# Softmax weights times values as one plain float32 product in both attentions of a two-layer hybrid step, with even and odd key tiles in the two column halves of TensorE

## The chip, the cores and the metric

The kernel runs on one core of a Trainium2 chip. The metric is the device time of one execution, in microseconds (us). The engines are called by their names in the profile: PE is TensorE's matrix multiply and PEld its weight load, DVE is VectorE, ACT is ScalarE, POOL is GpSimd, SP issues the transfers.

## What is computed

The program is one step of a two-layer backbone on 1024 latent tokens and 128 context tokens (1152 rows of width 1024). In every layer one input projection feeds three head groups, whose outputs go through an output projection, a LayerNorm, a SwiGLU feed-forward block (FFN) and another LayerNorm. The two attentions are what the change touches:

```python
# differential attention: 4 heads, queries and keys of 2 x 32, values of 64
s = jnp.einsum('bqhcd,bkhcd->bhcqk', qb, k).astype(F32) * scale
p = jax.nn.softmax(s, axis=-1)
a = p[:, :, 0] - lam * p[:, :, 1]
return jnp.einsum('bhqk,bkhd->bqhd', a.astype(v.dtype), v)
...
# latent attention (MLA): 8 heads, values of 64 made from a latent of 128
s = (jnp.einsum('bqhd,bkhd->bhqk', qn, k_nope)
     + jnp.einsum('bqhd,bkd->bhqk', qr, k_rope)).astype(F32) * scale
p = jax.nn.softmax(s, axis=-1)
return jnp.einsum('bhqk,bkhd->bqhd', p.astype(v.dtype), v)
```

The latent tokens see 1152 keys (9 tiles of 128), the context tokens only their own 128 (1 tile). All is float32.

## The kernel before

Most products are made in a split form: each float32 operand is written as a high and a low part in the type `fp32r` (helper `split`, lines 121 to 125: one engine copies the high part, another subtracts it from the source), and `mm3` (lines 127 to 130) adds three products: high times high, low times high, high times low. A product in `fp32r` is one matmul record on PE; a product in plain float32 is two records, one behind the other (the program has 296 matmuls on line 801, the trace 592 records).

A layer runs through these stages, each with its own tile pools: the input projection and the state-space part; the differential attention; the latent attention; output projection, norms and FFN. In a stage the work is written as a list of steps with due times (`weave`, which sorts them), and the tile framework's scheduler then sets the final order on each engine. The constants `LAG_D`, `AV_LAG_D`, `LAG_M`, `GSTEP`, `AV_LAG` are such due times, and the names ending in `BUFS` are buffer counts.

Differential attention, `diff_unit`: a unit is a head and two query tiles (256 queries; a unit of one tile for the context). `front` makes the scores of one tile and one of the two components (line 702, three matmuls of 384 keys into PSUM tile `s`, of which there are two), their maximum on DVE (line 714), the exponential on ACT (line 717, tile `e`), and after the second component the combination of both on POOL or DVE (lines 781 to 784). `tr` transposes `e` on PE (line 791, PSUM tile `t`, two buffers) and ACT copies the result to `aT` (line 794). `av` (line 801) multiplies the nine key tiles, one after the other, all into the same 64 rows of `o`, in plain float32: the values `vd` are the stationary operand (64 columns), `aT` streams 256 columns. `back_tokens` (line 809) transposes the 64-row result back with the identity.

Latent attention, `mla_unit`: a unit is again a head and two query tiles, 32 of them in a layer and 8 single context tiles. The scores are three-fold split products (line 702, tile `s`, 96 rows), with maxima on DVE (line 739), exponentials on ACT (line 748), and the division by the sum on POOL (line 959). `tr` transposes (line 967) and then splits the weights into `eh` and `el`: for three of five groups of two key tiles, ACT casts `eh` and DVE subtracts `el`, both from PSUM; for the groups 2 and 6, ACT copies to `ef`, DVE casts `eh`, POOL subtracts `el`. `av` (lines 986 and 987) uses stationary tiles `vv` of 128 columns, 64 for the high and 64 for the low part of the values, and streams first `eh` and then `el`, so each key tile takes two matmuls of 256 columns. At the end ACT copies the lower half of the result and DVE adds the upper (lines 990 and 991). `values` (line 899) makes `vv` and splits it on ACT and DVE.

Of the kernel before, what the change touches and what calls it, by code (L numbers as in the profile page):

```python
# [78 lines left out]
EL_BUFS = 4  # L79
EF_BUFS = 2  # L80
# [17 lines left out]
def dit_step(ctx, tc, ins, outs):  # L98
# [15 lines left out]
    def dma(out, in_):  # L114
        return sp.dma_start(out, in_)  # L115
# [31 lines left out]
    dma(ident, ins["ident"])  # L147
    mhalf = T(con, [128, 1], F32, "mhalf")
# [234 lines left out]
    for l in range(L):  # L383
# [375 lines left out]
        def diff_unit(h, t0, n, st):  # L759
# [46 lines left out]
            def back_tokens():  # L806
                o = v["o"][:, 256:256 + n * 64].rearrange("p (i d) -> p i d", d=64)
                for i in range(n):
                    pe.transpose(o[:, i], v["ob"][:, i * 128:(i + 1) * 128], ident[:64, :64])
# [89 lines left out]
        def values(half, kts, big):  # L899

            if half not in vv:
                vv[half] = T(mw["p"] if half else Vp, [128, 10, 4, 2, 64], F32R, f"vv{half}")
# [5 lines left out]
            p3 = ps.rearrange("p k (h d) -> p k h d", d=64)  # L908
            v = vv[half][:, kts[0]:kts[0] + n]
            split(v[:, :, :, 0, :], v[:, :, :, 1, :], p3, vec)  # L910
# [33 lines left out]
        def mla_unit(bi):  # L944
# [17 lines left out]
            def tr(g0):  # L962
# [6 lines left out]
                eh = T(mw["p"], [128, 512], F32R, "eh", EL_BUFS)  # L969
                el = T(mw["p"], [128, 512], F32R, "el", EL_BUFS)  # L970
                if g0 in (2, 6):
                    ef = T(mw["p"], [128, 512], F32, "ef", EF_BUFS)
                    act.copy(ef[:, :gn * w], pt[:, :gn * w])
                    split(eh[:, :gn * w], el[:, :gn * w], ef[:, :gn * w], pool, vec)
                else:
                    split(eh[:, :gn * w], el[:, :gn * w], pt[:, :gn * w], vec)
                v[g0] = (eh, el)

            def av(g0):
                if g0 == 0:  # L980
                    v["o"] = T(ps_pool[0], [128, 512], F32, "x", 1)[:, :w]
                eh, el = v[g0]
# [780 lines left out]
```

## Time and profile before

| | us |
|---|---|
| median of 3 runs | 3709.5 (3709.39, 3709.50, 4253.26) |
| the profiled execution's own time | 3713.83 |
| its span in the trace | 3711.8 |
| differential attention, layer 0 and layer 1 (first transpose on line 791 to first on line 967) | 263.0 and 228.9 |
| latent attention, layer 0 and layer 1 (first transpose on line 967 to last matmul on line 987) | 310.3 and 309.7 |

The busy shares of the engines are averages over stages with different limits, so the stages are read one by one. A matmul record lasts from when it is issued until its result is written, and records overlap: the cost of a matmul in a stream is the distance from its start to the start of the next, not its duration. An engine counts as busy during the whole record, so a busy PE can still be waiting for part of the time.

### The profile page before, as it was taken

The numbers are of one execution on the slowest core, as the hardware profiler recorded it, in microseconds if no ns is written. First come the engines' busy times: TensorE is split into PE (matmuls) and PEld (weight loads), VectorE is DVE, ScalarE is ACT, GpSimd is POOL, SyncE is SP. The second block draws the span as 40 slices with busy tenths as digits, with TensorE's granted clock in tenths as the row PEclk, the third lists the DMA queues.
The fourth block names the chain that finished last, engine by engine and source line by source line (L and its number), as shares of the span: only waits on it lengthen the run. The fifth ranks groups of instructions, "written<-read, shape, count | busy, mean of one in ns | idle before, by whom it ended". The sixth has DMA issues, their size and how long they took to land.

```text
span 3711.8 us, 54836 instructions
## 1 busy us (share of the span) xinstructions
PE 3432.9 (92%) x19856; PEld 3153.0 (85%) x19856; DVE 2124.9 (57%) x4285; ACT 1596.7 (43%) x3261; POOL 1540.0 (41%) x1583
## 2 busy tenths in 40 slices
PE   5898888999999999999998987899999999999997
PEld 2786447888988999999998965588889999999996
DVE  7865557888578465334465667688865321222336
ACT  2315556677563444444143265567755211111122
POOL 4561336677566555555034424467732101010013
PEclk8998999999999999999999988999999999999998
DMA  8665320011634333222135550001142211111112
GB/s 250 192 186 155 87 75 24 18 33 38 204 98 98 96 115 119 78 79 78 56 124 163 154 129 20 27 23 29 41 157 86 69 41 43 48 33 52 45 52 90
DMA packets 261694, 325.01 MB, mean 88 GB/s; under 512 B 65168, under 2 KB 206896, under 8 KB 261168
## 3 DMA queue, kind: packets, MB, share of 16 engines
q1 hardware_dynamic: 261424, 321.51, 29.6%
q8 instruction: 157, 2.57, 0.3%
q14 instruction: 113, 0.93, 0.1%
HBM read 261.71 MB, written 59.64 MB: 87 GB/s over the span
## 4 chain that ended last, share of the span: by engine, by line
PE 63%; DVE 11%; ACT 7%; DMA 5%; POOL 5%; issue 4%; SPq 1%; DVEq 0%; ACTq 0%; POOLq 0%
PE mm L130 14%; PE mm L129 14%; PE mm L128 13%; PE s L702 6%; PE t L801 3%; PE t L967 2%; POOL aa L255 2%; ACT e L717 1%; PE x L986 1%; PE t L791 1%; PE x L987 1%; DVE dm L714 1%; ACT e L748 1%; DVE mm L739 1%; SPq L115 1%
## 5 line engine op out<-in xcount | busy, mean ns | idle before, releaser
L128 PE MATMUL mm<-hh,wh 128*128 128x384 f32 x2784 | 947.0, 340 | 16.0 <-ACT wh L122 7.6
L130 PE MATMUL mm<-hh,wl 128*128 128x384 f32 x2784 | 945.7, 340 | 12.4 <-DVE wl L125 12.2
L129 PE MATMUL mm<-hl,wh 128*128 128x384 f32 x2784 | 944.8, 339 | 0.1
L128 PEld LDWEIGHTS mm<-hh,wh 128*128 128x128 f32 x2784 | 528.5, 190 | 19.0 <-ACT wh L122 9.5
L130 PEld LDWEIGHTS mm<-hh,wl 128*128 128x128 f32 x2784 | 528.3, 190 | 18.6 <-DVE wl L125 18.4
L129 PEld LDWEIGHTS mm<-hl,wh 128*128 128x128 f32 x2784 | 528.6, 190 | 0.5 <-POOL hl L125 0.4
L125 POOL TENSOR_TENSOR fl<-sg,fh 128x384 fp32r<-128x384 f32 x132 | 153.2, 1160 | 814.3 <-ACT fh L122 814.3
L122 ACT CAST wh<-wr 128x1024 fp32r<-128x1024 f32 (+2 forms) x302 | 239.9, 795 | 544.5 <-PE mm L129 489.7
L255 POOL TENSOR_TENSOR aa<-aa,at 128x256 f32<-128x256 f32 x392 | 328.0, 837 | 289.6 <-ACT at L254 264.1
L702 PE MATMUL s<-ks,qs 96*128 96x384 f32 (+2 forms) x1600 | 383.7, 364 | 56.7 <-ACT e L717 42.2
L125 DVE TENSOR_TENSOR wl<-wr,wh 128x1024 fp32r<-128x1024 f32 (+2 forms) x302 | 297.5, 985 | 231.4 <-ACT wh L122 223.6
L1112 DVE SCALAR_TENSOR_TENSOR acc<-mm,mods,acc 128x384 f32<-128x384 f32 (+2 forms) x640 | 309.4, 511 | 207.1 <-PE mm L130 205.0
L702 PEld LDWEIGHTS s<-ks,qs 96*128 96x128 f32 (+1 forms) x1600 | 276.2, 198 | 103.8 <-ACT e L717 57.7
L1221 DVE TENSOR_TENSOR sg<-mm,sg 128x384 f32<-128x384 f32 x132 | 73.3, 555 | 479.6 <-PE mm L130 453.5
L128 PE MATMUL mm<-fh,wh 128*128 128x384 f32 x960 | 324.3, 339 | 2.5 <-DVE acc L1112 1.9
L130 PE MATMUL mm<-fh,wl 128*128 128x384 f32 x960 | 320.4, 338 | 4.4 <-DVE wl L125 4.4
L129 PE MATMUL mm<-fl,wh 128*128 128x384 f32 x960 | 323.2, 337 | 0.0
L254 ACT ACTIVATE at<-aw,cond 128x256 f32<-128x256 f32 x392 | 199.3, 508 | 258.1 <-POOL aa L255 248.1
L714 DVE TENSOR_REDUCE dm<-s 128x1 f32<-128x1152 f32 (+1 forms) x148 | 181.5, 1237 | 95.5 <-PE s L702 95.2
L739 DVE TENSOR_REDUCE mm<-s 128x1 f32<-128x768 f32 (+2 forms) x264 | 189.4, 719 | 28.7 <-PE s L702 26.0
L959 POOL TENSOR_SCALAR e<-e,mr 128x1152 f32<-128x1152 f32 x144 | 168.8, 1175 | 83.5 <-DVE mr L958 56.6
L125 POOL TENSOR_TENSOR el<-ef,eh 128x512 fp32r<-128x512 f32 x128 | 164.5, 1286 | 80.4 <-DVE eh L124 75.1
(417 smaller groups left out, 6651.7 us busy)
## 6 DMA issues: line engine op xcount, KB each, us to landing
wr<-in_w_gu_dram SPq DMA_DIRECT2D x112, 512.0 KB, 3.6
aw<-in_w_ada_dram SPq DMA_DIRECT2D x224, 128.0 KB, 2.1
wr<-in_w_out_dram SPq DMA_DIRECT2D x48, 512.0 KB, 3.7
wr<-in_w_ada_dram SPq DMA_DIRECT2D x34, 512.0 KB, 5.3
wr<-in_w_dn_dram SPq DMA_DIRECT2D x112, 128.0 KB, 2.1
ks<-kd SPq DMA_DIRECT2D x64, 160.0 KB, 5.1
s_tb<-tbl SPq DMA_DIRECT2D x64, 145.0 KB, 3.4
qs<-qd SPq DMA_DIRECT2D x64, 144.0 KB, 3.9
```

The lines of the kernel that those rows point to most:

```text
L122: act.copy(hi, src)
L125: eng.tensor_tensor(lo, src, raw(hi), op=OP.subtract)
L128: pe.matmul(ps, wh, xh, start=first, stop=False)
L129: pe.matmul(ps, wh, xl, start=False, stop=False)
L130: pe.matmul(ps, wl, xh, start=False, stop=last)
L254: act.activation(t, w, AF.Copy, scale=sc)
L255: pool.tensor_tensor(a, a, t, op=OP.add)
L702: pe.matmul(out, q_ap[a], k_ap[b][:, k0:k0 + out.shape[-1]], start=i == 0, stop=i == len(passes) - 1)
L714: vec.tensor_reduce(m, s, op=OP.max, axis=AX.XY, negate=True)
L739: vec.tensor_reduce(m[:, j:j + 1], s, op=OP.max, axis=AX.XY, negate=True)
L959: pool.tensor_scalar(e[:, :nk], e[:, :nk], r, 1.0, op0=OP.mult, op1=OP.mult)
L1112: vec.scalar_tensor_tensor(acc[ch][m][:, a:b], ps[:, a:b], mods[l][:, gate + m, c:c + 1], acc[ch][m][:, a:b], op0=OP.mult, op1=OP.add)
```

## The change

Both attentions now multiply plain float32 weights with plain float32 values. The two key tiles of a pair go to the two halves of the PE array's columns: the even tile writes rows 0 to 63 of `o`, the odd one rows 64 to 127, each half accumulating for itself. In the latent attention the split of the weights disappears (`eh`, `el` and `ef` become one tile `aT` with one copy from PSUM, on DVE for groups 2 and 8 and else on ACT), and so does the split of the values. In the differential attention the sum of the two halves is made by `back_tokens`: a product with `id2`, two identities on top of each other, takes the place of the transposition. The latent attention still adds the halves on ACT and DVE.

```diff
-EL_BUFS = 4
+EL_BUFS = 6
...
+    id2 = T(con, [128, 64], F32, "id2")
+    vec.tensor_tensor(id2, ident[:, 0:64], ident[:, 64:128], op=OP.add)
...
-                    pe.matmul(o[0:64, 0:w], vd[:, kts[kt], h * 64:(h + 1) * 64], v[kt - j][:, j * w:(j + 1) * w],
-                              start=kt == 0, stop=kt == nkt - 1)
-                ob = v["ob"] = T(X, [64, 256], F32, "ob", 2)
-                act.copy(ob[:, :w], o[0:64, 0:w])
+                    pe.matmul(o[j * 64:(j + 1) * 64, 0:w], vd[:, kts[kt], h * 64:(h + 1) * 64],
+                              v[kt - j][:, j * w:(j + 1) * w], start=kt < 2, stop=kt >= nkt - 2)
+                m = min(nkt, 2) * 64
+                ob = v["ob"] = T(X, [128, 256], F32, "ob", 2)[0:m]
+                act.copy(ob[:, :w], o[0:m, 0:w])
...
-                    pe.transpose(o[:, i], v["ob"][:, i * 128:(i + 1) * 128], ident[:64, :64])
+                    pe.matmul(o[:, i], v["ob"][:, i * 128:(i + 1) * 128], id2[0:m], start=True, stop=True)
...
-                vv[half] = T(mw["p"] if half else Vp, [128, 10, 4, 2, 64], F32R, f"vv{half}")
+                vv[half] = T(mw["p"] if half else Vp, [128, 10, 256], F32, f"vv{half}")
...
-            split(v[:, :, :, 0, :], v[:, :, :, 1, :], p3, vec)
+            act.copy(vv[half][:, kts[0]:kts[0] + n], ps)
...
-                eh = T(mw["p"], [128, 512], F32R, "eh", EL_BUFS)
-                el = T(mw["p"], [128, 512], F32R, "el", EL_BUFS)
-                if g0 in (2, 6):
-                    ef = T(mw["p"], [128, 512], F32, "ef", EF_BUFS)
-                    act.copy(ef[:, :gn * w], pt[:, :gn * w])
-                    split(eh[:, :gn * w], el[:, :gn * w], ef[:, :gn * w], pool, vec)
+                aT = T(mw["p"], [128, 512], F32, "aT", EL_BUFS)
+                if g0 in (2, 8):
+                    vec.tensor_copy(aT[:, :gn * w], pt[:, :gn * w])
                 else:
-                    split(eh[:, :gn * w], el[:, :gn * w], pt[:, :gn * w], vec)
-                v[g0] = (eh, el)
+                    act.copy(aT[:, :gn * w], pt[:, :gn * w])
+                v[g0] = aT
...
-                    st = vv[h // 4][:, kts[g0 + j], h % 4].rearrange("p a d -> p (a d)")
-                    pe.matmul(o, st, eh[:, j * w:(j + 1) * w], start=g0 + j == 0, stop=False)
-                    pe.matmul(o, st, el[:, j * w:(j + 1) * w], start=False, stop=g0 + j == nkt - 1)
+                    kt = g0 + j
+                    pe.matmul(o[j * 64:(j + 1) * 64], vv[h // 4][:, kts[kt], h % 4 * 64:(h % 4 + 1) * 64],
+                              v[g0][:, j * w:(j + 1) * w], start=kt < 2, stop=kt >= nkt - 2)
```

Where the instructions stand. On PE in the latent attention of layer 0, near the end of one unit (`x` is the result of a unit, `s` scores, `vv` the values), the program of before has the two products of each key tile, which the scheduler puts apart as its queue allows:

```order
L986 MATMUL x_5918<-eh_5860,vv_1495_5549 128x256
L987 MATMUL x_5918<-el_5861,vv_1495_5549 128x256
L986 MATMUL x_5918<-eh_5860,vv_1495_5549 128x256
L987 MATMUL x_5918<-el_5861,vv_1495_5549 128x256
L986 MATMUL x_5918<-eh_5873,vv_1495_5549 128x256
L702 MATMUL s_1618_6017<-ks_5374,qs_5343 128x128
L702 MATMUL s_1618_6017<-ks_5375,qs_5343 128x128
L702 MATMUL s_1618_6017<-ks_5374,qs_5344 128x128
L987 MATMUL x_5918<-el_5874,vv_1495_5549 128x256
L986 MATMUL x_5918<-eh_5873,vv_1495_5549 128x256
```

In the changed program, near the end of a unit of the same head, each key tile has one matmul, an even and an odd one together (`x2`), between the projections of the next head (lines 128 to 130), transpositions and scores:

```order
L129 MATMUL t_5895<-qll_2892,wqh_5663 128x384
L130 MATMUL t_5895<-qlh_2891,wql_5664 128x384
L986 MATMUL x_5885<-aT_5883,vv_1496_5551 64x256 x2
L970 MATMUL t_5911<-ident_63,e_1527_5685 128x128
L970 MATMUL t_5911<-ident_63,e_1537_5723 128x128
L986 MATMUL x_5885<-aT_5893,vv_1496_5551 64x256 x2
L704 MATMUL s_1612_5992<-ks_5380,qs_5667 128x384
```

All 1184 matmuls of lines 986 and 987 become 592 on line 986, and these stand in 284 uninterrupted runs: 76 of one key tile, 160 of two, 46 of four, 2 of six. 206 runs come right behind a transposition.

On DVE at the same place, the program of before has subtractions (line 125) and casts (line 124) of the weights among the maxima (line 739):

```order
L125 TENSOR_TENSOR el_5824<-t_5820,eh_5823 128x256
L751 TENSOR_SCALAR ml_1572_5844<-ml_1572_5844 128x1
L958 RECIPROCAL mr_5848<-ml_1572_5844 128x1
L739 TENSOR_REDUCE mm_1584_5896<-s_1583_5892 128x1
L125 TENSOR_TENSOR el_5861<-t_5855,eh_5860 128x512
L742 TENSOR_SCALAR mn_1585_5899<-mm_1584_5896 128x1
L124 CAST eh_5873<-ef_5875 128x512
```

and the changed one has two copies for a unit:

```order
L974 COPY aT_5805<-t_5802 128x256
L753 TENSOR_SCALAR ml_1566_5824<-ml_1566_5824 128x1
L741 TENSOR_REDUCE mm_1575_5865<-s_1574_5861 128x1
L961 RECIPROCAL mr_5828<-ml_1566_5824 128x1
L974 COPY aT_5847<-t_5842 128x512
```

Five instructions of DVE for a unit become two; POOL's two subtractions go without a successor, and ACT has three copies where it had three casts and two copies.

In the differential attention the order on PE hardly moves. The end of the product of one unit before:

```order
L801 MATMUL t_3689<-aT_3646,vd_2888 64x256 x2
L801 MATMUL t_3689<-aT_3666,vd_2888 64x256 x2
L801 MATMUL t_3689<-aT_3671,vd_2888 64x256
L791 MATMUL t_3717<-ident_63,e_839_3557 128x128
L702 MATMUL s_889_3705<-ks_3478,qs_3477 128x384 x3
L702 MATMUL s_895_3724<-ks_3488,qs_3487 128x384 x3
L809 MATMUL t_3689<-ident_63,ob_3699 128x64 x2
```

and in the changed program, with the product that adds the halves in the place of the transposition:

```order
L804 MATMUL t_3691<-aT_3648,vd_2890 64x256 x2
L804 MATMUL t_3691<-aT_3668,vd_2890 64x256 x2
L804 MATMUL t_3691<-aT_3673,vd_2890 64x256
L793 MATMUL t_3719<-ident_63,e_840_3559 128x128
L704 MATMUL s_890_3707<-ks_3480,qs_3479 128x384 x3
L704 MATMUL s_896_3726<-ks_3490,qs_3489 128x384 x3
L814 MATMUL t_3691<-id_2_65,ob_3701 128x64 x2
```

There are 296 such matmuls before and after, in 64 runs before and 65 after; in each of the 32 units of two query tiles eight or nine key tiles stand together.

## Rows read from the trace of the kernel before

**Rows 1.** The page: busy time, share of the span and instructions of each engine.
```profile
PE 3432.9 (92%) x19856; PEld 3153.0 (85%) x19856; DVE 2124.9 (57%) x4285; ACT 1596.7 (43%) x3261; POOL 1540.0 (41%) x1583
```

**Rows 2.** Windows: latent attention (first two), differential attention; busy us, granted clock.
```profile
core 0: us, PE busy (x) PEld busy (x) DVE busy (x) ACT busy (x) POOL busy (x), PEclk, DMA share, GB/s
621.39:931.73 310.34, 289.01 (x1910) 261.64 (x1911) 257.99 (x601) 218.97 (x534) 213.42 (x186) 0.99 0.11 30
2418.83:2728.48 309.65, 286.70 (x1911) 260.24 (x1910) 259.52 (x602) 219.46 (x534) 213.75 (x187) 0.99 0.11 31
358.40:621.39 262.99, 228.06 (x1040) 139.34 (x1039) 157.45 (x263) 141.12 (x269) 105.72 (x69) 0.94 0.22 65
2189.90:2418.80 228.90, 189.99 (x927) 133.85 (x927) 157.31 (x248) 134.99 (x259) 104.64 (x69) 0.92 0.14 36
```

**Rows 3.** Chain that ended last, by line: differential attention layer 0, layer 1, latent attention.
```profile
by line: PE t L801 23.8%; PE s L702 16.7%; PE t L224 11.1%; PE t L791 8.7%; ACT e L717 7.0%; DMA wr<-in_w_ada_dram 6.5%; issue 4.8%; DVE dm L714 4.6%; ACT aT L794 3.5%; SPq L115 1.4%; PE s L128 1.2%; DVE wl L125 1.2%; DVE vv L125 1.1%; PE s
...
by line: PE t L801 18.6%; PE s L702 14.4%; ACT e L717 12.8%; DVE dm L714 10.5%; PE t L791 9.8%; issue 7.3%; DVE e L781 6.2%; ACT aT L794 3.8%; DVE roy L840 3.1%; PE s L128 1.8%; PE s L129 1.4%; PE s L130 1.4%; DVE otok L841 1.3%; DVE wl L77
...
by line: PE s L702 19.4%; PE t L967 12.8%; PE x L986 7.2%; PE x L987 7.1%; issue 6.8%; ACT e L748 5.9%; DVE mm L739 5.7%; DVE eh L124 3.9%; DVE el L125 3.3%; PE t L128 3.1%; ACT eh L122 2.6%; PE t L129 2.4%; PE t L130 2.3%; DVE ks L125 2.2%
```

**Rows 4.** Timeline of PE, float32 product of a differential unit: start, us, instructions.
```profile
484.48 3.67 PE L801 MATMUL t<-aT,vd 128*64 128x256 f32 x16 [0.51 <-ACT aT L794]
488.08 0.79 PE L702 MATMUL s<-ks,qs 128*128 128x384 f32 x3
488.80 0.65 PE L801 MATMUL t<-aT,vd 128*64 128x256 f32 x2
489.38 0.33 PE L791 MATMUL t<-ident,e 128*128 128x128 f32 x1
```

**Rows 5.** Timeline of PE, split product of a latent unit between its scores.
```profile
2599.59 1.21 PE L702 MATMUL s<-ks,qs 96*128 96x384 f32 x6
2600.63 0.28 PE L987 MATMUL x<-el,vv 128*128 128x256 f32 x1
2600.75 0.28 PE L986 MATMUL x<-eh,vv 128*128 128x256 f32 x1
2600.87 0.28 PE L987 MATMUL x<-el,vv 128*128 128x256 f32 x1
2600.99 0.28 PE L986 MATMUL x<-eh,vv 128*128 128x256 f32 x1
2601.11 0.34 PE L702 MATMUL s<-ks,qs 96*128 96x384 f32 x1
```

**Rows 6.** Chain in order of time, latent attention, transpositions: start, us, what.
```profile
2595.08 0.88 PE t L967 x8
...
2601.45 0.44 PE t L967 x4
```

**Rows 7.** Timelines of PE and PEld at line 270: four column groups together, one alone.
```profile
1092.36 0.26 PE L270 MATMUL lnw<-asum,id 128*32 128x16 f32 x8
...
1092.36 0.16 PEld L270 LDWEIGHTS lnw<-asum,id 128*32 128x32 f32 x8 [0.25 <-ACT acc L1159]
...
1241.23 0.23 PE L270 MATMUL lnw<-asum,id 128*32 128x16 f32 x2
...
1241.23 0.14 PEld L270 LDWEIGHTS lnw<-asum,id 128*32 128x32 f32 x2 [0.25 <-issue]
```

**Rows 8.** Groups by shape, latent attention of layer 0, PE: count, busy us, mean ns.
```profile
L702 PE MATMUL s<-ks,qs 96*128 96x384 f32 x534 | 120.5, 352 | 4.7 <-ACT e L748 3.6
L967 PE MATMUL t<-ident,e 128*128 128x128 f32 x584 | 90.0, 277 | 5.6 <-DVE ks L125 1.8 <-DVE el L125 1.6 <-ACT ef L973 0.8
L987 PE MATMUL x<-el,vv 128*128 128x256 f32 x288 | 79.4, 300 | 1.5 <-POOL el L125 1.1 <-DVE el L125 0.2
L986 PE MATMUL x<-eh,vv 128*128 128x256 f32 x288 | 78.7, 296 | 4.7 <-DVE ob L991 3.8 <-DVE eh L124 0.2 <-ACT eh L122 0.2
L128 PE MATMUL t<-qlh,wqh 128*128 128x384 f32 x40 | 14.5, 363 | 1.9 <-ACT ef L973 1.4 <-DVE vv L125 0.4
```

**Rows 9.** Groups by shape of the whole run, DVE, ACT and POOL.
```profile
L124 DVE CAST eh<-ef 128x512 fp32r<-128x512 f32 x128 | 89.3, 697 | 11.1 <-ACT ef L973 10.7
L125 DVE TENSOR_TENSOR el<-t,eh 128x512 fp32r<-128x512 f32 x128 | 87.0, 680 | 10.1 <-ACT eh L122 9.2
L125 DVE TENSOR_TENSOR el<-t,eh 128x256 fp32r<-128x256 f32 x64 | 26.9, 420 | 5.4 <-ACT eh L122 4.0
...
L973 ACT COPY ef<-t 128x512 f32<-128x512 f32 x128 | 75.6, 591 | 40.0 <-PE t L967 37.5 <-PE x L986 1.8
L122 ACT CAST eh<-t 128x512 fp32r<-128x512 f32 x128 | 75.2, 588 | 14.1 <-PE t L967 10.7 <-POOL el L125 1.7 <-PE x L986 0.7
...
L125 POOL TENSOR_TENSOR el<-ef,eh 128x512 fp32r<-128x512 f32 x128 | 164.5, 1286 | 80.4 <-DVE eh L124 75.1 <-DVE mr L958 3.8 <-PE t L130 1.5
```

**Rows 10.** Waits in the differential attention of layer 1: us in total, times, longest.
```profile
PEld s L702 <- ACT e L717: 32.5, 27, 3.8
```

More of the change, by code (lines that the diff above doesn't have):

```diff
@@ L800, in av @@
                     j = kt % 2
-                    pe.matmul(o[0:64, 0:w], vd[:, kts[kt], h * 64:(h + 1) * 64], v[kt - j][:, j * w:(j + 1) * w],
-                              start=kt == 0, stop=kt == nkt - 1)
-                ob = v["ob"] = T(X, [64, 256], F32, "ob", 2)
-                act.copy(ob[:, :w], o[0:64, 0:w])
+                    pe.matmul(o[j * 64:(j + 1) * 64, 0:w], vd[:, kts[kt], h * 64:(h + 1) * 64],
[3 more added lines that the diff above has]
+                act.copy(ob[:, :w], o[0:m, 0:w])
             def back_tokens():
+                m = min(nkt, 2) * 64
                 o = v["o"][:, 256:256 + n * 64].rearrange("p (i d) -> p i d", d=64)
                 for i in range(n):
-                    pe.transpose(o[:, i], v["ob"][:, i * 128:(i + 1) * 128], ident[:64, :64])
+                    pe.matmul(o[:, i], v["ob"][:, i * 128:(i + 1) * 128], id2[0:m], start=True, stop=True)
                 vec.tensor_tensor(otok[:, t0:t0 + n, h * 64:(h + 1) * 64], o,
@@ L907, in values @@
                     mw["wuvh"][:, c0:c0 + 256], mw["wuvl"][:, c0:c0 + 256], True, True)
-            p3 = ps.rearrange("p k (h d) -> p k h d", d=64)
-            v = vv[half][:, kts[0]:kts[0] + n]
-            split(v[:, :, :, 0, :], v[:, :, :, 1, :], p3, vec)
+            act.copy(vv[half][:, kts[0]:kts[0] + n], ps)
         qs = {}
@@ L981, in av @@
                     v["o"] = T(ps_pool[0], [128, 512], F32, "x", 1)[:, :w]
-                eh, el = v[g0]
                 o = v["o"]
                 for j in range(min(2, nkt - g0)):
-                    st = vv[h // 4][:, kts[g0 + j], h % 4].rearrange("p a d -> p (a d)")
-                    pe.matmul(o, st, eh[:, j * w:(j + 1) * w], start=g0 + j == 0, stop=False)
-                    pe.matmul(o, st, el[:, j * w:(j + 1) * w], start=False, stop=g0 + j == nkt - 1)
+                    kt = g0 + j
+                    pe.matmul(o[j * 64:(j + 1) * 64], vv[h // 4][:, kts[kt], h % 4 * 64:(h % 4 + 1) * 64],
+                              v[g0][:, j * w:(j + 1) * w], start=kt < 2, stop=kt >= nkt - 2)
                 if g0 + 2 >= nkt:
                     ob = T(mw["p"], [64, 256], F32, "ob", 2)[:, :w]
-                    act.copy(ob, o[64:128])
-                    vec.tensor_tensor(ob, o[0:64], ob, op=OP.add)
+                    if nkt > 1:
+                        act.copy(ob, o[64:128])
+                        vec.tensor_tensor(ob, o[0:64], ob, op=OP.add)
+                    else:
+                        act.copy(ob, o[0:64])
                     dma(MX[l][4 + h // 2, (h % 2) * 64:(h % 2 + 1) * 64, t0 * 128:t0 * 128 + w], ob)
```

## The prediction

> **What bounds the kernel now.** I read the page first. PE is busy for 92% of the span, DVE for 57% [rows 1]. That is an average, so the windows come next. The change touches four stretches: the latent attention of both layers (310.3 and 309.7 us) and the differential attention (263.0 and 228.9 us), together 1112 of 3712 us [rows 2]. In the latent stretch PE is busy 289 of 310 us and DVE 258; in the differential stretch of layer 1 PE is busy 190 of 229 us, and no other engine over 157 [rows 2]. The reader is to see two kinds of stage: one in which PE and DVE are both nearly full, and one in which nobody is full, so that the length is set by a loop of waits.
>
> A busy PE can wait, so I count its own work in one latent stretch from distances between starts. Six score matmuls take 1.04 us from 2599.59 to 2600.63, so 0.173 each; four split products take 0.48 us from 2600.63 to 2601.11, so 0.12 each [rows 5]; a transposition costs 0.11 [rows 6]. With the counts [rows 8] this is 534 x 0.173 = 92, 584 x 0.11 = 64, 576 x 0.12 = 69, and three lines of 40 projections at 0.173 = 21, together 246 us, and some 80 smaller records bring it to about 255. So about 55 of 310 us are waits of PE.
>
> The chain of waits tells what a shorter step is worth. In the differential stretch line 801 is 23.8% of the chain in layer 0 and 18.6% in layer 1: 62.6 and 42.6 us. In the latent stretch lines 986 and 987 are 14.3%, 44 us, and DVE's casts and subtractions of the weights 7.2%, 22 us [rows 3].
>
> **The change, part by part.**
>
> *Price of a plain float32 product.* Sixteen records take 3.60 us (484.48 to 488.08) and two take 0.58 (488.80 to 489.38), so a record in the stream costs 3.02/14 = 0.216 us, a key tile 0.43, against 2 x 0.12 = 0.24 for the split form [rows 4, 5]. A key tile alone is thus dearer than before, and only a pair whose halves run at once, 0.43 for two, breaks even.
>
> *Price of going to half the columns and back.* The run of two records takes 0.58, 0.15 more than 2 x 0.216; the three scores between two such runs take 0.72 (488.08 to 488.80) and not 3 x 0.173 = 0.52, so 0.20 more [rows 4, 5]. One round trip costs 0.35 us. The differential attention pays it today, in about as many runs as after. The latent attention pays nothing today, since its stationary tile has all 128 columns, and will pay it in 284 runs.
>
> *Do the halves run at once?* No row shows two column halves streaming 256 columns. The nearest is line 270, which fills four column groups of 32: its eight records take 0.26 us, where two records of a single group, elsewhere, take 0.23; the eight loads take 0.16 us and two take 0.14 [rows 7]. Four groups cost hardly more than one. The bounds are 0.43 us for a pair (at once) and 0.86 (one behind the other); I take 0.43, which the row is nearest to.
>
> *Latent attention, PE.* Removed: 1184 x 0.12 = 142 us in both layers. Added: 76 single tiles and 160 + 2 x 46 + 3 x 2 = 258 pairs, 334 x 0.43 = 144 us, and 284 round trips, 99 us. PE gets 101 us more, 50 a layer, and needs about 305 of the 310 us.
>
> *Latent attention, the others.* DVE loses 203 us of casts and subtractions and gets 64 large and 64 small copies back, which I price as the subtractions they resemble (0.68 and 0.42): 70 us. That is 66 us less a layer. POOL loses 164.5 us, 82 a layer. ACT loses 151 us of full-size casts and copies and 64 smaller ones, and gets 192 copies at 0.59, 113 us; about 30 us less a layer [rows 9]. The split of the values goes too, a few us. None of this is a gain by itself; it shortens PE's waits. The six buffers of `aT` (before four of each part) can't make a wait longer.
>
> *What the latent stretch does.* Two counts bound it. If PE's waits go entirely, it ends at 305, 5 us earlier; if they stay, at 360, 50 later. Between them I go by the chain: PE's product is on it for 44 of its 69 us, so 50 us more count as 50 x 44/69 = 32; DVE's 22 us there fall nearly away, because the copy feeds the product directly: take off 20. The stretch gets 12 us longer, to 322, which leaves PE 17 us of waits in place of 55, with DVE, POOL and ACT far from full. For two layers +24.
>
> *Differential attention.* In each of 32 units eight of nine tiles become four pairs, and each pair saves 0.43: 55 us, 27.6 a layer. PE spends 148 x 0.43 = 64 us a layer on line 801, and 62.6 and 42.6 of them are on the chain, so 27.0 and 18.4 us of the saving lie on it, 45 together. What is late next is the exponential: scores already wait 32.5 us for it in layer 1 [rows 10], and a PE that is done earlier meets it sooner. I keep three quarters: -34 us. The bounds are -55 and -10.
>
> *The sum of the halves.* 72 transpositions become products with two records each, every one with a full load of 128 columns, which I price as a transposition, 0.11: at most 72 x 0.11 = 8 us more, less what the old 64-row form cost in switching. I take +2, bounds -5 and +8. `id2` is one small DVE instruction at the start, hidden under the first loads.
>
> *Sum.* 3713.8 + 24 - 34 + 2 = 3705.8 us in the profile's own time. The median of the runs lies 4 us below that execution, so the forecast for the median is 3702 us: no change that a measurement of this kernel can tell, which I take to be 2%, or 74 us.
>
> **Rivals.**
>
> *The halves run one behind the other (slower).* Then each pair costs 0.86. The differential attention gains nothing (34 us back), and PE in the latent stretch needs 305 + 129 x 0.43 = 361 us a layer, more than the stretch has, so it becomes the bound there; all 111 us count. 3702 + 34 + 111 = 3847 us. Rows 7 speak against it, but with 16 columns a product, where little can collide. It decides if the first record of the odd tile starts two records behind the even one's. Chance 0.10.
>
> *The records stay in program order.* A tile's second pass cannot start before its first has streamed. If the odd tile's first pass must wait behind the even tile's second, a run of pairs takes one record more: 0.216 x (208 latent runs of two or more + 32 differential units) = 52 us, so about 3752. The Trainium skill says this of matmuls (TensorE: Matmul & The Clock Gate, "Part 3: Packing small matmuls — row/col tiling", what overlaps): they start and end strictly in program order; by that rule the time would be 3752. This trace disagrees for four small groups: with both loads of each group in order, the eight loads would stretch by the 0.03 us between a group's two loads, three times, to 0.23 us, and they took 0.16 [rows 7]. Chance 0.10.
>
> *PE's waits stay.* If the loop through scores, maximum, exponential and transposition rules, and not DVE's load, the latent stretch grows by the full 50 us a layer: 3702 + 76 = 3778. For it: lines 702, 967, 748 and 739 are 44% of the chain there [rows 3]. Against it: DVE is busy 258 of 310 us [rows 2], and loses a quarter of that. Chance 0.15.
>
> *The switches hide (faster).* PE waits 55 us in a latent stretch already; where a run of pairs would have waited for its weights anyway, the 0.35 us costs nothing. If half the switches go this way (25 us a layer) and the waits shrink as above, the latent stretch ends 13 us earlier in place of 12 later, and with the whole chain saving of 45 us the time is 3702 - 50 - 11 = 3641; with all 55 us, 3631. Chance 0.10.
>
> **How the numbers follow.** The forecast with its own spread, 3660 to 3745, has 0.55. From the others: 0.10 at 3847, 0.10 at 3752, 0.15 around 3778, 0.10 around 3636. Faster by over 2% is under 3635: half of the last rival and a little of the forecast's tail, 0.08. Slower by over 2% is over 3784: the first rival and 0.05 of the waits that stay, 0.15. Within 2%: 0.77. The range that leaves out 2 in 10 goes from 3638 to 3785.
>
> **What would show it.** In the changed trace line 986 should have 1184 records, and of a pair alone the four starts should lie within 0.3 us, with the next work of another shape 0.31 after the last. The run of 16 records on line 804 should take about 1.9 us in place of 3.6. The latent stretch should be 310 to 335 us with PE's idle time down, DVE near 190 and POOL near 130 us busy; the differential stretches should be 20 and 14 us shorter. I am wrong if a pair takes 0.86 us, if a latent stretch exceeds 345 us, or if the differential stretches do not move, which would mean that the exponentials set their length.

## The result, and the profile after

The changed kernel takes 3663.1 us (median of four runs, 3662.1 to 3666.0) against 3711.0 us for the kernel before on the same chip: a ratio of 0.9874, 95% interval 0.9854 to 0.9893. That is 1.3% faster, inside what a limit of 2% calls the same, inside the range (3638 to 3785), and 39 us below the forecast of 3702. One of the four executions of the kernel before, 4253.26 us, was a slow one: the ratio leaves it out, and goes by a median of 3709.5.

The profiled execution of the changed kernel took 3666.0 us, its span 3664.2. Its page, busy time and share of the span:

```profile
PE 3427.1 (94%) x19928; PEld 3041.6 (83%) x19928; DVE 1997.4 (55%) x4034; ACT 1541.3 (42%) x3133; POOL 1370.1 (37%) x1455
```

The windows, cut as in [rows 2], in order of time: differential attention and latent attention of layer 0, then of layer 1.

```profile
core 0: us, PE busy (x) PEld busy (x) DVE busy (x) ACT busy (x) POOL busy (x), PEclk, DMA share, GB/s
359.38:599.75 240.37, 206.69 (x1095) 128.29 (x1095) 157.53 (x268) 144.30 (x276) 109.27 (x71) 0.94 0.26 72
599.75:915.47 315.72, 308.65 (x1893) 218.80 (x1892) 199.17 (x471) 188.65 (x462) 125.75 (x120) 0.99 0.10 30
2165.38:2367.78 202.40, 169.93 (x983) 123.66 (x984) 149.58 (x255) 138.95 (x268) 107.28 (x71) 0.92 0.17 44
2367.78:2683.59 315.81, 308.42 (x1894) 218.84 (x1892) 198.70 (x471) 188.74 (x462) 126.02 (x120) 0.99 0.10 30
```

Against [rows 2], the differential stretches are 22.6 and 26.5 us shorter and the latent ones 5.4 and 6.2 us longer: -49.1 and +11.5. The remaining -10.0 of the span's -47.6 lie in the other three stretches, 8.3 of them between the two layers' attentions, where the change has no instruction. In the latent stretch DVE's busy time fell by 59 to 61 us, POOL's by 88, ACT's by 30, and PE's rose by 20 to 22: its idle time went from between 21 and 23 us to 7. On the page [rows 1] the totals of PE hardly differ, 3433 and 3427, because one stage lost what the other got.

These stretches are read from one execution each. The experiments ran in three sets on three chips, on which the kernel before had medians of 3709.8 to 3711.0 us. A kernel that differs from the changed one in nothing but four more buffers (the control below) has latent windows of 316.0 and 316.4 us, within 0.6 us of these.

The chain that ended last, by line, for the latent attention of layer 0 and the differential attention of layer 1, to be laid beside [rows 3]:

```profile
by line: PE s L704 30.6%; PE x L986 26.4%; PE t L970 20.4%; PE t L128 4.0%; PE t L129 3.1%; PE t L130 3.1%; issue 1.6%; DVE mm L741 1.3%; DVE aT L974 1.2%; ACT e L750 1.1%; DMA wr<-in_w_out_dram 1.1%; DMA pr<-mx 0.7%; DVE ks L125 0.7%; DVE 
...
by line: PE s L704 16.7%; ACT e L719 14.6%; DVE dm L716 13.7%; PE t L804 8.5%; PE t L793 8.3%; issue 6.3%; DVE e L783 3.9%; ACT aT L796 3.8%; POOL e L786 3.1%; DVE so L843 1.9%; PE s L128 1.7%; DVE ks L125 1.4%; DVE wl L781 1.4%; DVE roy L8
```

The latent stretch was a loop through PE, DVE and ACT; now six lines of PE are 88% of it, and no DVE line is over 1.3%. In the differential stretch the product fell from 18.6% to 8.5% of the chain, and scores, the exponential and the maximum lead.

The product itself, in the timeline of PE (start, duration, line, operation, shapes, count of records). Ahead of the dots stands a differential unit of nine tiles, behind them a latent unit's end:

```profile
442.90 1.95 PE L804 MATMUL t<-aT,vd 128*64 128x256 f32 x16 [0.28 <-ACT aT L796]
444.78 0.79 PE L704 MATMUL s<-ks,qs 128*128 128x384 f32 x3
445.50 0.65 PE L804 MATMUL t<-aT,vd 128*64 128x256 f32 x2
...
2601.58 1.84 PE L704 MATMUL s<-ks,qs 96*128 96x384 f32 x9
2603.26 0.38 PE L970 MATMUL t<-ident,e 128*128 128x128 f32 x2
2603.57 0.65 PE L986 MATMUL x<-aT,vv 128*64 128x256 f32 x4
2604.16 0.66 PE L970 MATMUL t<-ident,e 128*128 128x128 f32 x4
2604.74 0.65 PE L986 MATMUL x<-aT,vv 128*64 128x256 f32 x4
2605.33 0.80 PE L704 MATMUL s<-ks,qs 96*128 96x384 f32 x3
2605.96 0.60 PE L970 MATMUL t<-ident,e 128*128 128x128 f32 x4
2606.49 0.65 PE L986 MATMUL x<-aT,vv 128*64 128x256 f32 x2
2607.07 1.31 PE L704 MATMUL s<-ks,qs 96*128 96x384 f32 x6
```

Sixteen records take 1.88 us (442.90 to 444.78) where [rows 4] had 3.60. A latent pair of four records (2603.57 to 2604.16, 0.59) takes as long as a single tile of two (2606.49 to 2607.07, 0.58): the second half costs nothing. From the pair at 2603.57 to the next at 2604.74 are 1.17 us; the pair's 0.43 and four transpositions at 0.11 leave 0.30 for the round trip. From 2604.74 to 2606.49 are 1.75 us; 0.43, three scores at 0.173 and four transpositions leave 0.36.

### The profile page after: what moved, and what is told of

Read it like the earlier page. It is cut to its first block, busy times and chain, and to the rows that moved or that the text cites. A ratio compares the mean times of both kernels' runs of the same rounds, so it can differ in the third digit from the quotient of the medians.

```text
span 3664.2 us, 54318 instructions
## 1 busy us (share of the span) xinstructions
PE 3427.1 (94%) x19928; PEld 3041.6 (83%) x19928; DVE 1997.4 (55%) x4034; ACT 1541.3 (42%) x3133; POOL 1370.1 (37%) x1455
## 4 chain that ended last, share of the span: by engine, by line
PE 67%; DVE 11%; DMA 7%; ACT 5%; POOL 4%; issue 3%; SPq 1%; DVEq 0%; ACTq 0%; POOLq 0%
PE mm L130 14%; PE mm L129 14%; PE mm L128 14%; PE s L704 7%; PE x L986 5%; PE t L970 4%; ACT e L719 2%; DVE dm L716 1%; SPq L115 1%; PE t L804 1%; POOL aa L257 1%; PE t L793 1%; PE mm L544 1%; PE mm L543 1%; PE mm L542 1%
## 5 line engine op out<-in xcount | busy, mean ns | idle before, releaser
L750 ACT ACTIVATE e<-s,mn 128x384 f32<-128x384 f32 x248 | 181.6, 737 | 100.2 <-PE t L970 73.7
```

## The experiments

Two theories stand against each other. By mine, the latent stretch balances two things: PE's product gets dearer by two halves of 0.43 us for a pair and a switch of 0.35 us for each of 142 runs a layer, and DVE, ACT and POOL are relieved of the low part; the differential stretch takes only the cheaper pairs. The rivals deny one piece each: the halves don't overlap, the switches are hidden, or the relief is worth nothing.

**One half of the change alone.** First the differential part without the latent part, then the reverse.

```diff
 # differential part alone: latent attention as before
...
-                    pe.matmul(o[0:64, 0:w], vd[:, kts[kt], h * 64:(h + 1) * 64], v[kt - j][:, j * w:(j + 1) * w],
+                    pe.matmul(o[j * 64:(j + 1) * 64, 0:w], vd[:, kts[kt], h * 64:(h + 1) * 64],
...
 # latent part alone: differential attention as before
...
-                    pe.matmul(o, st, eh[:, j * w:(j + 1) * w], start=g0 + j == 0, stop=False)
-                    pe.matmul(o, st, el[:, j * w:(j + 1) * w], start=False, stop=g0 + j == nkt - 1)
+                    pe.matmul(o[j * 64:(j + 1) * 64], vv[h // 4][:, kts[kt], h % 4 * 64:(h % 4 + 1) * 64],
...
```

> The kernel before with the change in the differential attention alone. Theory A (the gain is the pairing of key tiles on the chain of the differential attention, and the latent part is by itself a small loss): the two differential stretches are 23 and 27 us shorter as in the changed kernel, the latent stretches stay at 310 us, and the time is about 3711 - 50 = 3661 us, no worse than the changed kernel. Rival B (the gain comes from the work that DVE, POOL and ACT lose, which lies in the latent attention): the differential stretches shorten by less than half of that, and the time is 3690 us or more.

> The changed kernel with the differential attention of before, so the change in the latent attention alone. Theory A: each latent stretch is 6 us longer than before, as in the changed kernel, and the time is 3711 + 12 = 3723 us. Rival B (lighter DVE, POOL and ACT pay off): 3695 us or less. A third case: about 10 us of the gain lie outside both attentions; if the latent part brings them, the time is 3711.

The differential part alone takes 3649.8 us (ratio 0.9844, 0.9826 to 0.9861), its stretches 239.4 and 201.6 us long. The latent part alone takes 3717.7 us (1.0022, 1.0010 to 1.0033), its latent stretches 317.1 and 317.2; the first of them is this window:

```profile
621.00:938.10 317.10, 310.05 (x1903) 220.34 (x1901) 200.72 (x476) 190.22 (x466) 127.03 (x121) 0.99 0.10 29
```

So the two parts have opposite signs, and each stretch moves by what its own part does, to within 4 us: the latent stretches of the differential part alone, which has no change there, are 307.1 and 308.2 us long, 3.3 and 1.4 under those of the kernel before. The changed kernel is not the best of the three. Half of it is faster by 13 us in the median; the two intervals overlap a little, but the latent windows, 307.1 and 308.2 us against 315.7 and 315.8, say the same. The third case, in which the latent part brings the 10 us outside both attentions, gets no support: with it alone the stretch between the layers' attentions stays at 1257.9 us.

**The halves.** Every key tile goes to the first column half, in both attentions. The latent attention leaves out the sum of the halves, and the differential one keeps its product with `id2`, over 64 rows; everything else is as in the changed kernel. Here is its latent part:

```diff
...
-                    pe.matmul(o[j * 64:(j + 1) * 64], vv[h // 4][:, kts[kt], h % 4 * 64:(h % 4 + 1) * 64],
-                              v[g0][:, j * w:(j + 1) * w], start=kt < 2, stop=kt >= nkt - 2)
+                    pe.matmul(o[0:64], vv[h // 4][:, kts[kt], h % 4 * 64:(h % 4 + 1) * 64],
+                              v[g0][:, j * w:(j + 1) * w], start=kt == 0, stop=kt == nkt - 1)
...
```

> The changed kernel with all key tiles, even and odd, in the first half of the columns, so that the products run one behind the other; the addition of the two halves at the end of a latent unit is left out, since there is one half only. Theory A (pairs run at once and PE bounds the latent stretch): each pair costs 0.43 us more; the differential stretches are back at 263 and 229 us, the latent ones grow by 129 x 0.43 = 56 us a layer to about 370, and the time is 3663 + 49 + 111 = 3823 us. Rival B (the product's form matters little, the other engines' load decides): under 3720 us.

It takes 3811.1 us (1.0282, 1.0263 to 1.0301). The windows of layer 0, differential and then latent:

```profile
360.90:621.50 260.60, 230.57 (x1086) 144.04 (x1086) 156.01 (x261) 142.31 (x272) 105.59 (x69) 0.96 0.23 66
621.50:986.70 365.20, 362.64 (x1903) 253.93 (x1901) 192.14 (x445) 189.26 (x465) 129.31 (x121) 1.00 0.09 26
```

Two runs of its product in the timeline of PE:

```profile
640.80 1.08 PE L986 MATMUL x<-aT,vv 128*64 128x256 f32 x4
641.81 1.34 PE L704 MATMUL s<-ks,qs 96*128 96x384 f32 x6
...
643.95 0.65 PE L986 MATMUL x<-aT,vv 128*64 128x256 f32 x2
```

Four records in one half take 1.01 us (640.80 to 641.81) and 0.59 in two. The differential stretch is back at its old length, and the latent one is 49.5 us longer than in the changed kernel, with PE busy 54 us more: 129 pairs at 0.42. (I expected 56 us a layer and 3823.) The halves overlap fully, and in both attentions that is what the float32 product lives on.

**The relief alone.** The kernel before, with the low part of the weights left out: one copy in place of the split, and both products read that copy. PE has the same work as before; DVE, ACT and POOL have about that of the changed kernel. The high parts get six buffers in place of four, as in the changed kernel, so what two more buffers are worth here is counted with the relief.

```diff
-EL_BUFS = 4
+EL_BUFS = 6
...
-                if g0 in (2, 6):
-                    act.copy(ef[:, :gn * w], pt[:, :gn * w])
-                    split(eh[:, :gn * w], el[:, :gn * w], ef[:, :gn * w], pool, vec)
+                if g0 in (2, 8):
+                    vec.tensor_copy(eh[:, :gn * w], pt[:, :gn * w])
                 else:
-                    split(eh[:, :gn * w], el[:, :gn * w], pt[:, :gn * w], vec)
-                v[g0] = (eh, el)
+                    act.copy(eh[:, :gn * w], pt[:, :gn * w])
+                v[g0] = (eh, eh)
```

> The kernel before, but in the latent attention the weights are not split: one copy from PSUM on ACT (DVE for groups 2 and 8) makes the high part, and both products read it, so the low part is left out of the result. PE has the same products as before and no change of column width; DVE, POOL and ACT lose what the changed kernel takes from them. It measures the relief alone. Theory A (the latent stretch has 55 us of PE waits, and the relief takes most of them): each latent stretch falls from 310 to 275 or 285 us, and the time to 3650 or 3670 us. Rival C (the waits belong to the loop of scores, maxima and exponentials and stay): 300 us or more a stretch, 3695 us or more in all.

It takes 3657.2 us (0.9859, 0.9836 to 0.9883). Its latent windows:

```profile
624.08:908.28 284.20, 271.60 (x1911) 258.41 (x1911) 201.77 (x497) 192.49 (x469) 129.51 (x121) 1.00 0.12 33
2393.93:2679.57 285.64, 272.80 (x1911) 259.84 (x1910) 202.08 (x497) 192.59 (x469) 129.84 (x122) 0.99 0.11 33
```

This splits the +5.4 and +6.2 us of the two layers. The relief takes off 26.1 and 24.0 us, and the step from this kernel to the changed one, which is the dearer product on PE (and the split of the values, a few us of other engines), puts 31.5 and 30.2 back. PE's product costs 49 us more by the count (-71 + 72 + 142 x 0.34), so by this estimate some 18 of it do not show in the time. PE's idle time falls only by 6 us in this step, from 12.6 and 12.8 to 7; the rest would be waits inside records that count as busy, since the profile models where a record ends.

The chain of this kernel in the latent attention of layer 0:

```profile
by line: PE s L702 31.4%; PE t L967 21.1%; PE x L983 10.5%; PE x L984 10.1%; PE t L128 3.5%; PE t L130 3.1%; PE t L129 3.1%; issue 3.0%; ACT e L748 2.8%; DVE rr L937 1.8%; ACT eh L973 1.5%; DVE q L936 1.2%; DVE mm L739 1.1%; POOL q L938 1.1
```

Against the third line of [rows 3], not only DVE's casts and subtractions are gone from it: the exponentials fell from 5.9% to 2.8% and the maxima on DVE from 5.7% to 1.1%.

**Fewer switches.** If 142 round trips a layer cost what they seem to, gathering them should pay. A unit's tiles are taken in falling order, so that the product starts only when its last weights are there and then runs through: one run for nine tiles (39 runs a layer), or two runs (71). A control has the ten buffers and nothing else.

```diff
-EL_BUFS = 6
+EL_BUFS = 10
...
-                for j in range(min(2, nkt - g0)):
-                    kt = g0 + j
+                for kt in kl:
+                    j = kt % 2
...
+            parts = [p for p in ([k for k in q if k < nkt] for q in ((8, 7, 6, 5, 4, 3, 2, 1, 0),)) if p]
...
+            for i, p in enumerate(parts):
+                back.append((LAG_M + (max(p) // 2 + AV_LAG) * GSTEP,
+                             lambda i=i, p=p: av(p, i == 0, i == len(parts) - 1)))
```

> The changed kernel, with the nine key tiles of a latent unit handed to the product together and in falling order, from tile 8 to tile 0, so that the product can start only when the last weights are there; ten buffers of aT in place of six. The tiles of a unit are then one run on PE: 78 runs in both layers in place of 284, 206 round trips fewer. Only the order of the summation differs. Theory A (a round trip costs PE 0.35 us, and about three fifths of what PE gained in this stretch lay on the path: 31 of 50 us a layer): 206 x 0.35 = 72 us less on PE, 45 us less in time, 3618 us, and each latent stretch at about 293 us; bounds 3591 and 3650. Rival B (the switches lay in waits of PE and were free, and a product that waits for the last group costs new ones): 3660 us or more, the latent stretches at 315 or above, PE's idle time in them up.

> The changed kernel, with the key tiles of a latent unit in two runs (3, 2, 1, 0 and then 8, 7, 6, 5, 4), each of which can start only when its last weights are there; eight buffers of aT. 142 runs in both layers in place of 284. Theory A: 142 x 0.35 = 50 us less on PE, three fifths of it in time, 31 us: 3632 us, about 300 us for a latent stretch, between the changed kernel and the kernel with one run. Rival B: no gain, 3655 us or more. If waiting for the last group costs as much as the switches, two runs come out ahead of one.

> A control: the changed kernel with ten buffers of aT in place of six and nothing else, since the kernel with one run has both. Theory A (the weights' buffers are not waited for in the changed kernel): within some 5 us of the changed kernel, 3663 us, the latent stretches at 315 to 316. Rival (the buffers gave what the kernel with one run gained): 3650 us, the latent stretches at 310.

One run takes 3649.8 us (0.9845, 0.9827 to 0.9863), two runs 3654.3 (0.9853, 0.9838 to 0.9868), the control 3664.6 (0.9870, 0.9848 to 0.9892). The buffers do nothing. The medians fall by 13 and 9 us, with intervals that overlap the changed kernel's; the latent windows show the gain more clearly, 309 and 311 us with one run, and 310.8 and 314.6 with two. It is a third of what I expected: theory A said 3618 for one run. And not all of the 13 is its own: of the 18.9 us between the two profiled executions the latent stretches bring 11.4, and 5.5 lie in the differential stretch of layer 1 (197.0 against 202.4), whose instructions are the same. The windows of the kernel with one run, latent attention of layers 0 and 1:

```profile
598.16:907.59 309.43, 285.09 (x1893) 228.01 (x1892) 196.94 (x471) 190.64 (x462) 126.13 (x121) 1.00 0.11 30
2355.44:2666.15 310.71, 285.25 (x1893) 228.13 (x1892) 196.93 (x471) 190.62 (x462) 125.95 (x120) 1.00 0.11 30
```

A piece of its timeline of PE, with a wait in brackets:

```profile
2606.68 0.79 PE L704 MATMUL s<-ks,qs 96*128 96x384 f32 x3 [0.81 <-ACT e L750]
2607.31 1.04 PE L970 MATMUL t<-ident,e 128*128 128x128 f32 x8
2608.28 2.37 PE L986 MATMUL x<-aT,vv 128*64 128x256 f32 x18
```

What PE waited for in its latent attention of layer 0 (us in total, times, longest):

```profile
PE s L704 <- ACT e L750: 7.7, 12, 0.8
PE t L970 <- DVE aT L974: 5.8, 5, 1.5
PE t L970 <- ACT aT L976: 5.2, 10, 1.0
```

The 103 round trips a layer that are gone were 36 us by the count. PE's busy time fell by 23 us a layer and its idle time rose by 17 to 18, from 7 to 24 or 25: 6.3 and 5.1 us are left. The waits are those of the loop, scores for the exponential and transpositions for the copies, which in layer 0 of the changed kernel were these:

```profile
PE t L970 <- DVE aT L974: 3.9, 6, 0.8
...
PE s L704 <- ACT e L750: 0.7, 2, 0.5
...
PE t L970 <- ACT aT L976: 0.3, 1, 0.3
```

**Where the run stands.** Is it the place of the run on PE that costs, or its 2.3 us, in which nothing else starts? The due time is moved towards the last transposition, and away from it.

```diff
-AV_LAG = 2.5
+AV_LAG = 0.5        # nearer; the other kernel: 6.0, with EL_BUFS = 12
```

> The kernel with one run of latent tiles, with the product's due time moved nearer to its last transposition: AV_LAG 0.5 in place of 2.5 steps. PE's own work is the same. Theory A (the run of nine tiles costs waits because of where it stands on PE: 309 us with some 272 of own work): if nearness to the last copy is what costs, the latent stretch grows beyond 309 us, to 315 or more. Rival (the waits come from the length of the burst, 2.3 us in which no score and no transposition starts): no change, 309 to 311 us, 3650 us in all.

> The kernel with one run of latent tiles, with the product's due time moved away from its last transposition: AV_LAG 6.0 in place of 2.5 steps, and twelve buffers of aT. Theory A (nearness to the last copy): PE's waits in the latent stretch fall from 37 us towards 17, the stretch to some 295 us, 3620 us in all. Rival (the length of the burst): 309 to 311 us, 3650 us in all.

Nearer takes 3672.5 us (0.9894, 0.9874 to 0.9913), its latent stretches 317.8 and 318.5. Later takes 3659.3 (0.9861, 0.9843 to 0.9878); its latent windows:

```profile
599.76:910.86 311.10, 286.09 (x1893) 228.30 (x1892) 196.80 (x471) 191.10 (x462) 126.35 (x121) 1.00 0.11 30
2362.16:2678.14 315.98, 290.38 (x1894) 231.11 (x1892) 196.81 (x471) 191.16 (x462) 126.11 (x120) 0.98 0.10 29
```

PE is idle 25 us in each of these two. Nearer, the stretch grows by 8 us, as theory A said; later gains nothing, against theory A's 295 us, and the second window is above the rival's 311 as well. So nearness costs when it is less than here, but is not what keeps these waits; that agrees with the length of the burst, which none of these kernels changes alone, so it is not proved.

**The same in the differential attention**, where tile 8 often stands in a run by itself ([rows 4] show one): falling order there, once on the kernel with one latent run, once on the differential part alone.

```diff
-                for kt in range(nkt):
+                for kt in reversed(range(nkt)):
...
-                              v[kt - j][:, j * w:(j + 1) * w], start=kt < 2, stop=kt >= nkt - 2)
+                              v[kt - j][:, j * w:(j + 1) * w], start=kt >= nkt - 2, stop=kt < 2)
```

> The kernel with one run of the latent tiles, and in the differential attention too the nine tiles from 8 down to 0, so that tile 8 no longer stands in a run by itself: 40 runs in place of 65 in both layers. Theory A: 25 x 0.35 = 9 us less on PE than with one latent run alone, since the whole of PE's saving came through in this stretch: 4 us off each differential stretch, 3609 us. Rival B: the product of the first eight tiles now waits for the exponential and the transpositions of tile 8, and the differential stretches stay at 240 and 202 us or grow.

> The kernel with the differential part alone (the latent attention as before, with weights in two parts), with the nine tiles of a differential unit in falling order, so that they stand in one run. Theory A: 4 us less in each differential stretch than with the differential part alone, 3641 us; the latent stretches stay at 307 to 310 us. Rival B: no gain or a loss, 3650 us or more. The difference of this kernel to the one with both attentions in one run is then the worth of the latent part once its switches are gone: by theory A that part ends some 32 us ahead.

Both lose: 3691.5 us (0.9955, 0.9942 to 0.9967) and 3672.8 (0.9903, 0.9884 to 0.9921), 42 and 23 us above their counterparts, not 9 below. The differential window of layer 0, first of the differential part alone, without the falling order:

```profile
361.30:600.67 239.37, 203.56 (x1085) 128.00 (x1085) 161.76 (x268) 143.94 (x275) 107.25 (x70) 0.95 0.25 72
```

The same window with the falling order:

```profile
357.63:621.82 264.19, 214.33 (x1094) 134.08 (x1094) 159.44 (x270) 144.80 (x276) 108.13 (x70) 0.90 0.23 65
```

PE's wait for the exponential in it, without the falling order:

```profile
PE s L704 <- ACT e L719: 12.4, 16, 2.3
```

And with it:

```profile
PE s L704 <- ACT e L719: 27.0, 29, 3.3
```

Rival B holds: a product that waits for the ninth tile holds up the scores behind it, and PE's wait for the exponential doubles. The wait is not the whole of the 24.8 us. The granted clock (the column PEclk, a share of the full 2.4 GHz) fell with it, from 0.95 to 0.90. Taken times that clock, the windows are 227 and 238 us of full clock, so the clock can account for at most some 14 of the 24.8 us (an estimate); whether the waits brought it down is not shown.

In layer 1 the falling order on the differential part alone lost only 2 us. The windows of layer 1, first without the falling order, then with it on the differential part alone, then with it on the kernel with one latent run:

```profile
2161.81:2363.38 201.57, 170.25 (x981) 126.93 (x980) 148.64 (x256) 137.98 (x266) 106.56 (x71) 0.90 0.17 43
...
2181.11:2384.67 203.56, 166.92 (x977) 120.50 (x978) 150.66 (x256) 138.44 (x268) 107.14 (x70) 0.92 0.17 43
...
2194.58:2412.57 217.99, 172.61 (x984) 126.85 (x984) 150.55 (x257) 138.96 (x268) 110.77 (x71) 0.88 0.16 41
```

The first two differ little in time, but the clock was higher in the second, which hides a part of the loss: PE's wait for the exponential rose there too, from 15.7 to 23.2 us. In the third the layer lost 21 us against its counterpart (196.95 us at a clock of 0.92). So the order costs in both layers, and how much depends on the granted clock of the execution as well; the third is from the slowest of ten executions, 3709.1 us where the median is 3691.5.

## Why the prediction was right, and where it was off

The forecast said no change by 2%, and that is what came; its sum was 40 us too high (3705.8 against the profiled 3666.0), so the verdict came out right with a sum that overrated the loss in one part and underrated the gain in the other. Term by term, of these 40:

- **The price of a product, and the halves: right.** A record is 0.216 us, a pair 0.43, sixteen records 1.88 us where I expected 1.9. The rival with serial halves (3847) is the kernel with one half, which came at 3811; it falls for the changed kernel. Its sum was off as well: it adds all 111 us to stretches of 322 us, though its own count has PE need 361 us a layer; with 361 as the length it gives 3702 + 34 + 78 = 3814. The rival of records in program order (3752; 3702 + 52 is 3754) falls too: distances between starts of the changed kernel's records on line 986 have a median of 7 ns, since the first records of both tiles of a pair start together, and then the second ones. The Trainium skill (TensorE: Matmul & The Clock Gate, "Part 3: Packing small matmuls — row/col tiling") says that matmuls start and end in strict program order. The trace fits that if the two records of a float32 product count as one matmul, and the price that I drew from it, each record in turn, did not come: 0.59 us for a pair and 0.58 for a single tile.
- **The switch: right.** I took 0.35 us; the changed kernel shows 0.30 between transpositions and 0.36 with scores between. The Trainium skill (TensorEngine Tiling (Array Packing), "Tiling Modes") says that a change of tiling mode drains TensorE, and gives no time for it. The trace shows that each change costs the times above, which fits; it does not show a drain as such. The number of runs, 142 a layer, is what I counted.
- **The dearer product in the latent stretch: right in size, in part by luck.** 50 us more on PE, weighted by the chain to 32; measured 31.5 and 30.2. But the weight, 44 of 69 us, is from the chain before the relief. In the kernel with the relief alone, to which the 31 us are added, lines 983 and 984 are 20.6% of the chain, 59 of the 69 us, and that share would have made it 42. Used once more, for the kernel with one run, three fifths of PE's saving failed: 45 us expected, 13 measured.
- **The relief there: mis-sized.** "DVE's 22 us there fall nearly away ... take off 20": 26.1 and 24.0. I counted only DVE's casts and subtractions in the chain; ACT's cast, at 2.6% of 310 us another 8 us in [rows 3], and the maxima and exponentials, whose shares fell too in the kernel with the relief alone, I left at nothing. With the relief at 25 the latent term is +7 a layer and not +12; measured +5.4 and +6.2. That is 12.5 us of the 40. PE was idle 7 us in the window, and its lines are 88% of the chain: the stretch is PE's now. The 17 us of waits that I left it were more than it had.
- **The differential term: mis-sized, and the largest miss.** "I keep three quarters: -34 us", since scores would wait longer for the exponential. They did not. PEld's wait for it in layer 1, 32.5 us in [rows 10], is now

```profile
PEld s L704 <- ACT e L719: 27.2, 34, 2.5
```

  and the stretches gave 49 us of the 55 that the pairs save, more even than the 45 on the chain. By layers the chain was less good: 22.6 us where it had 27.0, and 26.5 where it had 18.4. [rows 10] shows that there was a wait, not that it would grow, and the size of the discount had no row behind it. 15 us of the 40.
- **The sum of the halves: a little off.** I took +2 for it. A transposition before and its product after both take 0.11 us from start to start, and the term can't be told from zero. 2 us.
- **10 us in stretches that the change does not touch: most of them go with the granted clock; why that differed is open.** The stretch between the layers' attentions, before and after:

```profile
931.73:2189.90 1258.17, 1205.77 (x7021) 1177.96 (x7021) 696.88 (x1418) 549.83 (x1075) 599.32 (x734) 0.97 0.39 114
915.47:2165.38 1249.91, 1195.34 (x7019) 1169.70 (x7018) 695.08 (x1415) 548.30 (x1074) 597.88 (x734) 0.98 0.39 115
```

  It was 1249 to 1258 us long in all thirteen profiled kernels, and its length goes with the granted clock: in the traces the clock stood at its lower level, 1.2 GHz, for 75 us of it before and for 51 us after, and over the thirteen the two have a correlation of 0.94. The control with ten buffers, which is the changed kernel there, had 64 us at the lower level and 1253.7 us. It was longest in the kernel before and with the latent part alone (1257.9), but shortest, 1248.9, in the kernel with one half, whose differential stretches have the old length; so the runs do not show that the change moves it. Executions of the kernel before differ by 15 us among themselves (3699.5 to 3714.7 in one set). I had no term for it.

The rival in which the switches hide (3641) came nearer than the forecast, 22 us below the measured time where that was 39 above, because it took the whole chain saving in the differential attention. Its latent part was wrong: 13 us earlier a layer, where 5.4 and 6.2 later were measured. Some of the product's cost does hide, 18 of 49 us by the count, against the 25 us a layer of this rival; the runs do not tell whether it is the switches or the records that hide. The rival in which PE's waits stay (3778) fell with the idle time of 7 us.

No kernel here beats the differential part alone (3649.8); one latent run on top of it ends at the same 3649.8. In its stretches the float32 product with one run still costs a little, 309.4 and 310.7 us against 307.1 and 308.2; in the whole time it can be told neither as a cost nor as a gain.

## What to carry to other kernels

A chain's share is a first price and no more: it put the dearer product at 32 us where 31 were measured, and the gathered one at 45 where 13 were. Once a part of the change has moved the chain, the share has to be read again. Take relief from all engines that lose work, not from one, and don't discount a saving for a wait that no row shows growing. When a change has parts in different stretches, price and run them apart: one part gave 60 us here, 51 of them in its own stretches, and the other took some of it back. Look at the granted clock of each stretch before putting a difference down to the kernel. Fewer switches or fewer waits is a choice: gathering a product into one run saves the switches, but holds up what stands behind it on PE.

## What the runs showed of the hardware

- Two column halves with plain float32 operands run at once: 0.43 us for two tiles of 256 columns, the same as for one. I had only the four groups of 16 columns in [rows 7] to go by.
- The switch's price sits in several places: the next record of another shape starts 0.309 us after the last one of the half, 0.093 more than a record; the first record of a run takes 0.267 in place of 0.216; the first half-column record starts 0.268 after a score where a transposition starts 0.178 after it; and behind the run the first score takes 0.281 in place of 0.175, or the first transposition 0.165 in place of 0.109 (medians of the changed kernel's distances between starts).
- In the kernel with one run, work taken off PE came back as time only in part: 23 us less busy time a layer became 17 or 18 us of waits and 5 or 6 us of gain.
- A stretch of 1250 us that the change does not touch was 1249 to 1258 us long, with 50 to 75 us at the lower clock of 1.2 GHz.
